# Second norm of a fused backbone layer: four MLP chunks split during the projection, its last four chunks worked token tile by token tile, three products kept back, and a fixed order

## The chip, the core and the metric

The kernel is one program on one core of a Trainium2 chip. It is written against a scheduling framework: the program is written as a stream of operations on named tiles, and the framework decides each engine's order of instructions and places the semaphores, except for operations that are pinned to the order in which they are written. The engines are TensorE (PE, with its weight loads shown as PEld), VectorE (DVE), ScalarE (ACT), GpSimd (POOL) and SyncE (SP, which here only issues the loads). The metric is the device time of one execution in microseconds, as the median of several runs.

## The reference

One layer of a diffusion backbone on 256 latent tokens of width 2048, with 256 context tokens: an attention branch and a pooling branch are merged by gates, projected by `w_o`, and followed by an MLP of width 8192. Everything is float32. The end of it, which is where the change lies:

```python
        mix = token_mixer(q, k_all, v_all, p[..., P_OFF:G_OFF], p[..., G_OFF:], lam, lam_init,
                          subln_w[l], pool_w[l], pool_scale[l], w_a_up[l], w_b_up[l], w_o[l])
        x = x + ga * mix
        x = x + gm * sq_relu_mlp(modulate(x, norm_mlp_w[l], sm, cm), w_ff1[l], w_ff2[l])
```

`token_mixer` ends with `(g_a * y_a + g_b * y_b) @ w_o`, `modulate(x, w, shift, scale)` is `rmsnorm(x, w) * (1 + scale) + shift`, and `sq_relu_mlp(h, w1, w2)` is `square(relu(h @ w1)) @ w2`. The vectors `ga`, `sm`, `cm` and `gm` are pieces of one product of the conditioning vector with a large weight `w_mod`. The second norm needs the whole row of 2048 features of `x`, so nothing of the MLP can start before the last column of the projection is done.

## The kernel before

**Tiles.** The 256 tokens are two token tiles of 128 (called token 0 and token 1, `t` in the code). A product of full precision is made of three products of a faster type: each operand is split into a high piece (a cast) and a low piece (the rest), and high x high, high x low and low x high are summed. Each weight comes as chunks of 128 x 1024 (512 KB). A chunk is loaded by SP into one of five `raw` buffers, its high piece is cast by ACT and its low piece subtracted by DVE (`load_next`, lines 196 to 240); the pieces lie in three buffers each (`whi`, `wlo`). A `raw` buffer is free for the next load once DVE has made the low piece. `wchunk` hands out the chunks in the order of the list `stream` and loads some ahead.

**The projection.** `w_o` is done in four groups `g` of 512 columns, each with eight chunks (called projection chunks 0 to 7; two slices of 128 features each) and one PSUM bank per token tile, `wo`. `xstat` (line 423) issues for each chunk twelve products of 512 columns: eight with the weight's high piece and four with its low piece, for both token tiles. The chunks of the last `last` of a group are instead worked token by token: first all products of token 0, then all of token 1. Before, `last` is 3 for the last group.

**The second norm.** `projected` (line 905) takes a finished bank: multiply by `ga` (tile `xtmp`), add to the residual `x1`, square on ACT with a row sum. `scaled` multiplies the new `x1` by the norm's scale into `yt`, 512 columns at a time. `norm2` sums the row sums of a token tile and makes the inverse root with two table functions on ACT and three tiny operations on DVE. `shifted(kp)` applies the root and adds the shift on one pair of feature slices (256 columns, "feature pair" `kp`, 0 to 7). `hidden2(kp)` turns that pair with PE transposes into the PSUM tile `h2T`, and `split` makes its high piece on ACT and its low piece on DVE, into `h2`.

**The first eighth of the MLP.** `ff1_first` (line 955) computes 1024 of the 8192 hidden features with the tokens as the stationary operand, from sixteen chunks of `w_ff1a` (MLP chunks 0 to 15, one slice of 128 features each). `products(k, t)` issues six products of 512 columns for chunk `k` and token tile `t`: three for each half `h` of the columns, into four banks `f1_{t}{h}` (shown as `f`).

**What sets the order.** While `ordered` is set, every operation of ACT and DVE that goes through the wrapper `Engine` is pinned, and its line reads L67; `ordered_pe` does the same for PE. Before, PE is pinned only in the last token-by-token group of the projection, and ACT and DVE are pinned from `projected(3, 0, ...)` to the second `products(1, 1)`. Operations of helpers that were bound before the flag was set, and all others, are placed by the framework. Between these stages run the late vectors: `late_gen` loads the weights of `ga`, `cm`, `sm` and `gm` in parts of 512 KB through the same `raw` buffers, one part whenever the `rate` of the chunks that were loaded has summed to one, and DVE multiplies and adds each part into `macc` (line 636). Before, `gm`, which is needed only at the very end, begins during the projection.

Of the kernel before, what the change touches and what calls it, by code (L numbers as in the profile page):

```python
# [17 lines left out]
P = 128  # L18
# [30 lines left out]
def layer(ctx: ExitStack, tc, a, out):  # L49
# [36 lines left out]
    def pairtile(name):  # L86
        return s16(name, [P, 2, 8, T], F32R)

    late = [None]
    credit = [0.0]  # L90
    credit_rate = [0.0]
# [81 lines left out]
    FIRST_AHEAD = 6  # L173
    x1s = []
    first = []

    def x1_tile():
        if not x1s:
# [17 lines left out]
    def load_next():  # L196
# [24 lines left out]
        raw = raw_chunk(src, n)  # L221
        if key == ("w_ff1a", 0):
            hi, lo = (pool.tile([P, n], F32R, tag="aT", name=nm, bufs=2) for nm in ("hi0", "lo0"))
        elif key == ("w_ff1a", 1):
            halves = [[work(nm, dt=F32R) for nm in ("hi1", "lo1")] for _ in range(2)]
            for h in range(2):
                split(*halves[h], raw[:, h * 512:h * 512 + 512])
            loaded.append((key, *zip(*halves)))
            return
        else:  # L230
            hi = pool.tile([P, n], F32R, tag="whi", name="whi", bufs=3)
            lo = pool.tile([P, n], F32R, tag="wlo", name="wlo", bufs=3)
# [4 lines left out]
        credit_rate[0] = rate  # L237
        while credit[0] >= 1.0:
            credit[0] -= 1.0
            next(late[0], None)  # L240

    def wchunk(*key, ahead=AHEAD):
        while len(loaded) < min(done[0] + 1 + ahead, len(stream)) or loaded[done[0]][1] is None:
# [179 lines left out]
    def xstat(w, banks, toks, nk=8, last=1, more=0):  # L423

# [3 lines left out]
        for ch in range(nk - last + 1):  # L428
# [6 lines left out]
            for group in groups:  # L435
                for part in range(2):
                    for i, kk, t in group:
                        k = 2 * (ch + i) + kk
                        h, tt = toks[t]
                        wt = chunks[i][part][:, kk * 512:kk * 512 + 512]  # L440
                        if part == 0:
                            pe.matmul(banks[t], tok(h, k, 0, tt), wt, start=k == 0, stop=False)  # L442
                            pe.matmul(banks[t], tok(h, k, 1, tt), wt, start=False, stop=False)  # L443
                        else:
                            pe.matmul(banks[t], tok(h, k, 0, tt), wt, start=False, stop=k == 2 * nk - 1)  # L445
            yield len(banks)
# [146 lines left out]


    ga_bc = s8("ga_bc", [P, D])
    mods = {}
    parts = []

    def late_gen():
        for name in ("ga", "cm", "sm", "gm"):  # L600
            if name == "ga":
                dst = ga_bc
            elif name == "gm":
                mods["gm"] = s8("gm_bc", [P, D])
                dst = mods["gm"]
            else:
                if "sb" not in mods:
                    mods["sb"] = s16("sb", [P, 2, D])
                dst = mods["sb"][:, 0 if name == "cm" else 1, :]
# [306 lines left out]
    def norm2(t):  # L916
        rv = small("rv", 1)
        vec.reduce_sum(rv, ssq[:, 4 * t:4 * t + 4], axis=AX.X)
        r2[t] = rsq(rv, 1, 1.0 / D)

    for g in range(4):
# [8 lines left out]
        next(late[0])  # L930
    flush()

    h2 = [pairtile(f"h2_{i}") for i in range(2)]
# [21 lines left out]
    def ff1_first(wo):  # L955
# [5 lines left out]
        bs = [[bank(f"f1_{t}{h}") for h in range(2)] for t in range(2)]  # L961
        chunks = {}

        def products(k, t):
            hi, lo = chunks[k]
            for h in range(2):
# [24 lines left out]
        scaled(3)  # L991
        shifted(2)
        hidden2(2)
        products(2, 1)
        for k in range(3, KT):
            if k % 2 == 0 and k < 14:
                shifted(k // 2 + 1)
                hidden2(k // 2 + 1)
            chunks[k] = wchunk("w_ff1a", k)
            for t in range(2):  # L1000
                products(k, t)
        at = pairtile("act")
# [177 lines left out]
```

## Time and profile before

| what | value |
|---|---|
| median of three runs | 1474.42 us |
| lowest and highest run | 1473.76 and 1475.06 us |
| the profiled execution's own time | 1475.86 us |
| its span, first to last instruction | 1474.0 us |
| PE busy | 1440.5 us, 98% of the span |
| DVE, ACT and POOL busy | 1000.8, 684.3 and 121.3 us |
| mean granted clock of PE | 0.990 |

A profile's timeline gives for each row the start and length in microseconds, the engine, the line of the kernel, the operation, what it writes and reads by the program's tile names, the shapes, how many equal ones are merged, and in square brackets how long the engine was idle before it and what released it. A table of stretches gives, for each stretch of time, each engine's busy time with its number of instructions, the clock that PE was granted, the share of the sixteen DMA engines that was busy, and GB/s. PE's ends are modelled: the next product starts before the shown end of the one ahead of it, so its pace is read from starts.

### The profile page before, as it was taken

Reading aid. Unit: us, or ns where it says so; the run is one execution under the profiler, and the core shown is the slowest. Engines: PE = TensorE matmul, PEld = TensorE weight load, DVE = VectorE, ACT = ScalarE, POOL = GpSimd, SP = SyncE. Lnnn points to the kernel's source line nnn. Section 1 sums busy time; section 2 is a strip of 40 time slices with the busy share of each in tenths; the row PEclk is TensorE's granted clock in tenths of the full one; section 3 lists DMA queues with packets and bytes.
Section 4 is the critical chain, followed back from the end, with each engine's and each line's share of the span. In section 5 each row is a group of like instructions: output and inputs, shape, how many; then the busy total and the mean of one; then the engine's idle time right before and its main releaser. Section 6 shows DMA issues by size and latency. Waiting matters only on the chain.

```text
span 1474.0 us, 19772 instructions
## 1 busy us (share of the span) xinstructions
PE 1440.5 (98%) x7466; PEld 1186.7 (81%) x7466; DVE 1000.8 (68%) x1243; ACT 684.3 (46%) x929; POOL 121.3 (8%) x120
## 2 busy tenths in 40 slices
PE   4999999999999999999999999999999999999998
PEld 2667887778878888888878888888888888888887
DVE  4667786768887687778776755666665555555675
ACT  4334346466554444544444555445354454544442
POOL 0001110101400000000001000001000000000260
PEclk7999999999999999999999999999999999999999
DMA  9996685435788879798746776677765655566554
GB/s 380 401 407 224 203 287 167 143 114 165 234 284 294 301 279 301 278 330 294 252 146 222 233 237 226 234 239 240 238 230 186 193 192 189 191 193 191 186 195 141
DMA packets 97440, 347.85 MB, mean 236 GB/s; under 512 B 11073, under 2 KB 11713, under 8 KB 97345
## 3 DMA queue, kind: packets, MB, share of 16 engines
q1 hardware_dynamic: 96768, 345.51, 69.4%
q8 instruction: 58, 0.95, 0.3%
q0 software_dynamic: 576, 1.08, 0.2%
q14 instruction: 38, 0.30, 0.1%
HBM read 344.45 MB, written 2.10 MB: 235 GB/s over the span
## 4 chain that ended last, share of the span: by engine, by line
PE 88%; DVE 6%; ACT 2%; DMA 2%; issue 1%; POOL 0%; DVEq 0%; SPq 0%; ACTq 0%; POOLq 0%
PE f L1029 14%; PE f L443 8%; PE f L442 8%; PE f L445 8%; PE f L1032 7%; PE pg L443 3%; PE pg L442 3%; PE pg L445 3%; PE w_k L67 3%; PE wo L442 2%; PE wo L445 2%; PE wo L443 2%; PE pyy L445 2%; PE pyy L442 2%; PE pyy L443 2%; DVE wlo L234 2%
## 5 line engine op out<-in xcount | busy, mean ns | idle before, releaser
L234 DVE TENSOR_TENSOR wlo<-raw,whi 128x1024 fp32r<-128x1024 f32 (+1 forms) x433 | 538.4, 1245 | 349.1 <-ACT whi L233 324.1
L233 ACT CAST whi<-raw 128x1024 fp32r<-128x1024 f32 (+1 forms) x433 | 452.8, 1047 | 555.6 <-PE f L443 184.6
L1029 PE MATMUL f<-h,whi 128*128 128x512 f32 x896 | 224.3, 392 | 0.0
L443 PE MATMUL f<-whi,act 128*128 128x512 f32 x512 | 199.3, 389 | 0.0
L442 PE MATMUL f<-whi,act 128*128 128x512 f32 x512 | 199.2, 389 | 0.0
L1029 PEld LDWEIGHTS f<-h,whi 128*128 128x128 f32 x896 | 161.8, 189 | 29.6
L636 DVE SCALAR_TENSOR_TENSOR macc<-raw,sil,macc 128x1024 f32<-128x1024 f32 x128 | 165.0, 1289 | 3.3 <-issue 2.6
L445 PE MATMUL f<-wlo,act 128*128 128x512 f32 x512 | 136.8, 389 | 0.0
L1032 PEld LDWEIGHTS f<-h,wlo 128*128 128x128 f32 x896 | 122.2, 190 | 8.7
L1032 PE MATMUL f<-h,wlo 128*128 128x256 f32 x896 | 124.9, 282 | 0.0
L445 PEld LDWEIGHTS f<-wlo,act 128*128 128x128 f32 x512 | 96.1, 188 | 19.9
L443 PEld LDWEIGHTS f<-whi,act 128*128 128x128 f32 x512 | 96.2, 188 | 19.8
L442 PEld LDWEIGHTS f<-whi,act 128*128 128x128 f32 x512 | 96.2, 188 | 19.7
L442 PE MATMUL pg<-whi,hL 128*128 128x512 f32 x256 | 101.4, 396 | 0.0
L443 PE MATMUL pg<-whi,hL 128*128 128x512 f32 x256 | 100.6, 393 | 0.0
L1040 POOL TENSOR_TENSOR rsq<-relu 128x512 f32<-128x512 f32 x28 | 29.2, 1042 | 543.3 <-ACT relu L1039 523.0
L445 PE MATMUL pg<-wlo,hL 128*128 128x512 f32 x256 | 68.6, 390 | 0.0
L443 PEld LDWEIGHTS pg<-whi,hL 128*128 128x128 f32 x256 | 48.5, 189 | 10.4 <-issue 0.2
L442 PEld LDWEIGHTS pg<-whi,hL 128*128 128x128 f32 x256 | 48.5, 189 | 10.3 <-issue 0.2
L445 PEld LDWEIGHTS pg<-wlo,hL 128*128 128x128 f32 x256 | 48.3, 189 | 10.2
L617 POOL MEMSET macc<- 128x1024 f32 x8 | 7.6, 955 | 461.6 <-DVE al L260 357.1
L442 PE MATMUL wo<-whi,mix 128*128 128x512 f32 x116 | 45.2, 390 | 0.0
(263 smaller groups left out, 2083.4 us busy)
## 6 DMA issues: line engine op xcount, KB each, us to landing
raw<-in_w_ff_dram SPq DMA_DIRECT2D x240, 512.0 KB, 4.0
raw<-in_w_m_dram SPq DMA_DIRECT2D x64, 512.0 KB, 9.7
raw<-in_w_ga_dram SPq DMA_DIRECT2D x32, 512.0 KB, 4.6
raw<-in_w_cm_dram SPq DMA_DIRECT2D x32, 512.0 KB, 4.4
raw<-in_w_gb_in_dram SPq DMA_DIRECT2D x32, 512.0 KB, 4.7
raw<-in_w_ga_in_dram SPq DMA_DIRECT2D x32, 512.0 KB, 5.0
raw<-in_w_sm_dram SPq DMA_DIRECT2D x32, 512.0 KB, 4.8
raw<-in_w_o_dram SPq DMA_DIRECT2D x32, 512.0 KB, 5.2
```

Of the source, the lines that this page charges most:

```text
L67: return (lambda *a, **k: pin(emit(*a, **k))) if self.flag[0] else emit
L233: act.copy(hi, raw)
L234: vec.tensor_sub(lo, raw, hi.bitcast(F32))
L442: pe.matmul(banks[t], tok(h, k, 0, tt), wt, start=k == 0, stop=False)
L443: pe.matmul(banks[t], tok(h, k, 1, tt), wt, start=False, stop=False)
L445: pe.matmul(banks[t], tok(h, k, 0, tt), wt, start=False, stop=k == 2 * nk - 1)
L617: gp.memset(acc, 0.0)
L636: pin(vec.scalar_tensor_tensor(acc, raw, sil[:, 0, k:k + 1], acc, ALU.mult, ALU.add))
L1029: pe.matmul(ps, hi[:, kk * P:kk * P + P], both(h2, k), start=k == 0, stop=False)
L1032: pe.matmul(ps[:, T:2 * T], lo[:, kk * P:kk * P + P], act_slice(h2, k, 0), start=False, stop=k == KT - 1)
L1040: gp.tensor_mul(sq, r, r)
```

## The change

The last group of the projection works its last four chunks (4 to 7) token by token instead of three. Chunk 4 gets pieces of its own (`pair`), so that its split does not wait for one of the three `whi` and `wlo` buffers. Of the MLP, four chunks instead of two are loaded and split before the norm begins; chunks 2 and 3 get a 16 KB tile of their own, `early`. Of token 1's projection the last three products (those with the weight's low piece for the last three feature slices) are kept back and issued between the transposes of token 0's feature pairs 0 and 1. The low pieces of those two pairs are made only after both transposes have been issued. After that, token 0 is multiplied with MLP chunks 0 to 3, with token 1's transposes inside the last of them, and then token 1. The pinned stretch of ACT and DVE now reaches to feature pair 2, the kept-back products stay pinned on PE, and every `shifted` is pinned wherever it stands. The second half of `h2` is taken when it is first needed, and `gm` is begun only with the chunks of the MLP. `scaled(3)` moves from behind `projected` to behind token 1's second pair.

```diff
@@ load_next @@
         if key == ("w_ff1a", 0):
             hi, lo = (pool.tile([P, n], F32R, tag="aT", name=nm, bufs=2) for nm in ("hi0", "lo0"))
+        elif key == ("w_o", 3, 4):
+            pair = s8("pair", [P, 2, 1024], F32R)
+            hi, lo = pair[:, 0, :], pair[:, 1, :]
+        elif key in (("w_ff1a", 2), ("w_ff1a", 3)):
+            i = 2 * (key[1] - 2)
+            if i == 0:
+                early.append(s16("early", [P, 4, 1024], F32R))
+            hi, lo = early[0][:, i, :], early[0][:, i + 1, :]
...
         while credit[0] >= 1.0:
             credit[0] -= 1.0
-            next(late[0], None)
+            if "gm" not in mods or mods["gm"] is not None or key[0] in ("w_ff1a", "w_ff1"):
+                next(late[0], None)
@@ xstat @@
+                        elif held_back is not None and group is groups[-1] and k >= 2 * nk - 3:
+                            held_back.append(partial(pe.matmul, banks[t], tok(h, k, 0, tt), wt, start=False,
+                                                     stop=k == 2 * nk - 1))
                         else:
                             pe.matmul(banks[t], tok(h, k, 0, tt), wt, start=False, stop=k == 2 * nk - 1)
@@ late_gen @@
             elif name == "gm":
+                mods["gm"] = None
+                yield
                 mods["gm"] = s8("gm_bc", [P, D])
@@ the projection @@
-        for ch, _ in enumerate(xstat(("w_o", g), bs, [(mix, 0), (mix, 1)], last=3 if g == 3 else 1, more=2 if g == 3 else 0)):
-            ordered_pe[0] = g == 3 and ch == 4
+        for ch, _ in enumerate(xstat(("w_o", g), bs, [(mix, 0), (mix, 1)], last=4 if g == 3 else 1, more=4 if g == 3 else 0,
+                                     held_back=held_back if g == 3 else None)):
+            ordered_pe[0] = g == 3 and ch == 3
@@ shifted, hidden2 @@
-            vec.scalar_tensor_tensor(yt[:, t, fs], yt[:, t, fs], r2[t], mods["sb"][:, 1, fs], ALU.mult, ALU.add)
+            pin(nc.vector.scalar_tensor_tensor(yt[:, t, fs], yt[:, t, fs], r2[t], mods["sb"][:, 1, fs], ALU.mult, ALU.add))
 
     def hidden2(kp, ts=(0, 1)):
+        turned2(kp, ts)()
+
+    def turned2(kp, ts):
+        if kp // 4 == len(h2):
+            h2.append(pairtile("h2_1"))
         pt = bank("h2T")
...
-        split(ht[:, 0, k8:k8 + 2, sl], ht[:, 1, k8:k8 + 2, sl], pt.rearrange("p (a t) -> p a t", t=T)[:, :, sl])
+        src = pt.rearrange("p (a t) -> p a t", t=T)[:, :, sl]
+        hi = ht[:, 0, k8:k8 + 2, sl]
+        act.copy(hi, src)
+        return lambda: vec.tensor_sub(ht[:, 1, k8:k8 + 2, sl], src, hi.bitcast(F32))
@@ ff1_first @@
+        for k in range(4):
+            chunks[k] = wchunk("w_ff1a", k, ahead=0)
         projected(3, 0, wo[0])
         norm2(0)
         shifted(0, (0,))
-        hidden2(0, (0,))
-        chunks[0] = wchunk("w_ff1a", 0, ahead=1)
-        products(0, 0)
+        shifted(1, (0,))
+        low = [turned2(0, (0,))]
+        for emit in held_back:
+            emit()
+        low.append(turned2(1, (0,)))
+        for emit in low:
+            emit()
         projected(3, 1, wo[1])
-        shifted(1, (0,))
-        hidden2(1, (0,))
-        chunks[1] = wchunk("w_ff1a", 1, ahead=1)
-        products(1, 0)
         norm2(1)
+        for k in range(3):
+            products(k, 0)
+        products(3, 0, (0,))
         shifted(0, (1,))
-        chunks[2] = wchunk("w_ff1a", 2, ahead=0)
-        products(2, 0)
+        shifted(1, (1,))
         hidden2(0, (1,))
-        products(0, 1)
-        shifted(1, (1,))
+        products(3, 0, (1,))
         hidden2(1, (1,))
-        products(1, 1)
-        ordered[0] = ordered_pe[0] = False
+        chunks[4] = wchunk("w_ff1a", 4, ahead=0)
+        for k in range(2):
+            products(k, 1)
         scaled(3)
         shifted(2)
         hidden2(2)
-        products(2, 1)
-        for k in range(3, KT):
+        ordered[0] = ordered_pe[0] = False
+        for k in range(2, 4):
+            products(k, 1)
+        for k in range(4, KT):
```

How this moves instructions is read from the built programs, engine by engine; the numbers behind tile names count buffers. PE at the end of the projection before (`wo_6357` is token 0, `wo_6358` token 1):

```order
L67 MATMUL wo_6357<-whi,mix_4785 128x512 x12
L67 MATMUL wo_6357<-wlo,mix_4785 128x512 x6
L67 MATMUL wo_6358<-whi,mix_4785 128x512 x12
L67 MATMUL wo_6358<-wlo,mix_4785 128x512 x6
L944 MATMUL h2T<-prm,yt 128x128 x2
L263 MATMUL f_00_6517<-hi_6464,h_0_6514 128x512
```

And in the changed kernel (`wo_6341` is token 0, `wo_6342` token 1):

```order
L67 MATMUL wo_6341<-pair,mix_4785 128x512 x2
L67 MATMUL wo_6341<-wlo,mix_4785 128x512 x6
L67 MATMUL wo_6342<-pair,mix_4785 128x512 x4
L67 MATMUL wo_6342<-whi,mix_4785 128x512 x12
L67 MATMUL wo_6342<-pair,mix_4785 128x512 x2
L67 MATMUL wo_6342<-wlo,mix_4785 128x512 x3
L966 MATMUL h2T<-prm,yt 128x128 x2
L67 MATMUL wo_6342<-wlo,mix_4785 128x512 x3
L966 MATMUL h2T<-prm,yt 128x128 x2
L274 MATMUL f_00_6505<-hi_6435,h_0_6503 128x512
```

Token 1 has 24 products instead of 18 here, of which 21 stand ahead of token 0's first transposes and three between them and the second pair. The next place is DVE from the last weight splits to token 1's multiply. Before:

```order
L260 TENSOR_TENSOR lo_6473<-raw,hi_6472 128x512
L234 TENSOR_TENSOR wlo<-raw,whi 128x1024
L67 TENSOR_TENSOR xtmp<-wo_6357,ga_bc 128x512
L67 TENSOR_TENSOR x_5801<-xtmp,x_5801 128x512
L903 TENSOR_TENSOR yt<-x_5801,sb 128x512
L67 TENSOR_REDUCE rv<-ssq_5820 128x1
...
L67 SCALAR_TENSOR_TENSOR yt<-yt,rq_y,sb 128x256
L938 SCALAR_TENSOR_TENSOR yt<-yt,rq_y,sb 128x256 x3
L67 TENSOR_TENSOR h_0_6514<-h2T,h_0_6514 128x2x128
L67 TENSOR_TENSOR xtmp<-wo_6358,ga_bc 128x512
```

And in the changed kernel:

```order
L271 TENSOR_TENSOR lo_6444<-raw,hi_6443 128x512
L244 TENSOR_TENSOR wlo<-raw,whi 128x1024
L244 TENSOR_TENSOR early<-raw,early 128x1024 x2
L67 TENSOR_TENSOR xtmp<-wo_6341,ga_bc 128x512
L67 TENSOR_TENSOR x_5801<-xtmp,x_5801 128x512
L67 TENSOR_REDUCE rv<-ssq_5820 128x1
...
L955 SCALAR_TENSOR_TENSOR yt<-yt,rq_y,sb 128x256 x2
L67 TENSOR_TENSOR h_0_6503<-h2T,h_0_6503 128x2x128 x2
L67 TENSOR_TENSOR xtmp<-wo_6342,ga_bc 128x512
```

The two early splits now stand between the projection's last split and token 0's multiply, the shifts of later features (L938) and `scaled(3)` (L903) have left the stretch, and token 1's multiply stands behind both low pieces instead of one.

More of the change, by code (lines that the diff above doesn't have):

```diff
@@ L87, in pairtile @@
         return s16(name, [P, 2, 8, T], F32R)
+    mods = {}
     late = [None]
@@ L175, in layer @@
     first = []
+    early = []
     def x1_tile():
@@ L421, in xmm, with xstat @@
             mm3(ps, tok(h, k, 0, t), tok(h, k, 1, t), hi[:, sl], lo[:, sl], first, last)
-    def xstat(w, banks, toks, nk=8, last=1, more=0):
+    def xstat(w, banks, toks, nk=8, last=1, more=0, held_back=None):
         for ch in range(nk - last + 1):
@@ L595, in layer @@
     ga_bc = s8("ga_bc", [P, D])
-    mods = {}
     parts = []
@@ L919, in norm2 @@
         r2[t] = rsq(rv, 1, 1.0 / D)
+    held_back = []
     for g in range(4):
         bs = [bank(f"wo{t}") for t in range(2)]
-        for ch, _ in enumerate(xstat(("w_o", g), bs, [(mix, 0), (mix, 1)], last=3 if g == 3 else 1, more=2 if g == 3 else 0)):
-            ordered_pe[0] = g == 3 and ch == 4
+        for ch, _ in enumerate(xstat(("w_o", g), bs, [(mix, 0), (mix, 1)], last=4 if g == 3 else 1, more=4 if g == 3 else 0,
+                                     held_back=held_back if g == 3 else None)):
+            ordered_pe[0] = g == 3 and ch == 3
         if g < 3:
@@ L931, in layer @@
     flush()
-    h2 = [pairtile(f"h2_{i}") for i in range(2)]
+    h2 = [pairtile("h2_0")]
     def shifted(kp, ts=(0, 1)):
@@ L962, in ff1_first, with products @@
         chunks = {}
-        def products(k, t):
+        def products(k, t, hs=(0, 1)):
             hi, lo = chunks[k]
-            for h in range(2):
+            for h in hs:
                 whi, wlo = (w[h] if isinstance(w, tuple) else w[:, h * 512:h * 512 + 512] for w in (hi, lo))
                 mm3(bs[t][h], tok(h2, k, 0, t), tok(h2, k, 1, t), whi, wlo, k == 0, k == KT - 1)
+        for k in range(4):
+            chunks[k] = wchunk("w_ff1a", k, ahead=0)
         projected(3, 0, wo[0])
@@ L998, in ff1_first @@
                 hidden2(k // 2 + 1)
-            chunks[k] = wchunk("w_ff1a", k)
+            if k > 4:
+                chunks[k] = wchunk("w_ff1a", k)
             for t in range(2):
```

## The prediction

> **What bounds the kernel now.** I read the page first: TensorE (PE) is the bound, so only time in which PE does not run at its full pace can be won.
>
> ```profile
> span 1474.0 us, 19772 instructions
> PE 1440.5 (98%) x7466; PEld 1186.7 (81%) x7466; DVE 1000.8 (68%) x1243; ACT 684.3 (46%) x929; POOL 121.3 (8%) x120
> ```
>
> Then the table of stretches around the second norm, cut at the events of the next view (columns: stretch, its length, busy time of each engine with instructions, granted clock, DMA share, GB/s).
>
> ```profile
> 743.22:751.38 8.16, 8.16 (x37) 6.57 (x35) 4.33 (x10) 1.66 (x5) 0.00 (x0) 1.00 0.66 243
> 751.38:755.00 3.62, 3.02 (x13) 2.19 (x13) 3.62 (x9) 0.60 (x2) 0.00 (x0) 1.00 0.00 0
> 755.00:758.50 3.50, 1.58 (x7) 0.76 (x5) 3.21 (x8) 3.11 (x6) 0.00 (x0) 1.00 0.00 0
> 758.50:762.00 3.50, 3.49 (x8) 2.80 (x9) 3.40 (x8) 1.08 (x3) 0.00 (x0) 0.51 0.67 202
> ...
> 766.44:772.00 5.56, 5.56 (x30) 4.67 (x29) 3.00 (x3) 3.17 (x4) 0.00 (x0) 1.00 0.07 10
> ```
>
> PE is full until 751.38 and again from 766.44. Between them it loses time in two ways: it waits, and for 3.5 us its clock is 0.51. PE's own timeline names the waits (start, length, what, idle before and its releaser):
>
> ```profile
> 743.22 2.88 PE L67 MATMUL wo<-whi,mix 128*128 128x512 f32 x12
> 745.94 1.52 PE L67 MATMUL wo<-wlo,mix 128*128 128x512 f32 x6
> 747.30 2.88 PE L67 MATMUL wo<-whi,mix 128*128 128x512 f32 x12
> ...
> 751.68 0.44 PE L944 MATMUL h2T<-prm,yt 128*128 128x128 f32 x2
> 752.58 0.50 PE L263 MATMUL f<-hi,h 128*128 128x512 f32 x1 [0.46 <-ACT h L67]
> ...
> 757.25 0.73 PE L263 MATMUL f<-whi,h 128*128 128x512 f32 x2 [1.41 <-ACT whi L67]
> 758.51 0.80 PE L264 MATMUL f<-wlo,h 128*128 128x512 f32 x1 [0.52 <-DVE wlo L67]
> ...
> 763.33 0.50 PE L263 MATMUL f<-hi,h 128*128 128x512 f32 x1 [0.46 <-ACT h L67]
> ...
> 764.83 0.38 PE L944 MATMUL h2T<-prm,yt 128*128 128x128 f32 x2
> ...
> 765.28 0.39 PE L264 MATMUL f<-lo,h 128*128 128x512 f32 x1
> ```
>
> Twelve products start every 2.72 us (743.22 to 745.94): 0.227 each. A pair of transposes with the product behind it takes 0.45 (764.83 to 765.28), so a pair costs 0.22. The MLP products of the gap, counted by the same table for the tile f alone:
>
> ```profile
> 751.38:766.44 15.06, 11.03 (x36) 7.57 (x36) 0.00 (x0) 0.00 (x0) 0.89 0.32 106
> ```
>
> At full pace 36 products (8.16) and four pairs (0.88) take 9.04 us; they took 15.06. **The stage loses 6.02 us**, the most that can be won here. Of it the eight products at half clock (758.50 to 762.00) are 8 x (0.43 - 0.227) = about 1.7; the rest is waiting.
>
> What PE waits for shows in VectorE's (DVE's) timeline: first token 0's norm, then weights whose splits stand behind it.
>
> ```profile
> 747.50 0.69 DVE L67 TENSOR_TENSOR xtmp<-wo,ga_bc 128x512 f32<-128x512 f32 x1 [2.67 <-PE wo L67]
> ...
> 751.14 0.48 DVE L67 SCALAR_TENSOR_TENSOR yt<-yt,rq_y,sb 128x256 f32<-128x256 f32 x1
> ...
> 752.73 0.42 DVE L67 TENSOR_TENSOR h<-h2T,h 128x256 fp32r<-128x256 f32 x1
> ...
> 757.24 1.22 DVE L67 TENSOR_TENSOR wlo<-raw,whi 128x1024 fp32r<-128x1024 f32 x1
> ...
> 758.45 2.35 DVE L234 TENSOR_TENSOR wlo<-raw,whi 128x1024 fp32r<-128x1024 f32 x2
> ...
> 761.29 0.48 DVE L67 SCALAR_TENSOR_TENSOR yt<-yt,rq_y,sb 128x256 f32<-128x256 f32 x1
> ```
>
> ScalarE (ACT) copies the turned tile in between:
>
> ```profile
> 752.15 0.37 ACT L67 CAST h<-h2T 128x256 fp32r<-128x256 f32 x1 [1.63 <-PE h2T L944]
> ```
>
> From the first multiply (747.50) to the shifted tile (751.14 + 0.48) a norm takes 4.12; from a transpose (751.68) to the first product that uses it (752.58) 0.90. The chunks split at 757.24 and 758.45 hold PE up (1.41 and 0.52), and token 1's norm stands in the same queues: its shift comes at 761.29.
>
> **The change part by part.** I set out the new order on before's clock. No product is added or removed; PE is full up to the projection's last group, so that group's start moves by one chunk (12 products) to 743.22 - 2.72 = 740.50.
>
> *Four last chunks token by token, and the kept-back products.* Token 0's 24 products end at 740.50 + 24 x 0.227 = 745.94. Its multiply started 0.20 after the group's end before (747.50 against 747.30), so now at 746.14; the first shifted tile is ready at 750.26, the second 0.40 later. Token 1's first 21 products cover until 750.70: the transposes find their tile ready, with 0.44 to spare. The three kept-back products (0.68) and the second pair then cover the 0.90 that the first piece needs for its copy: the first MLP product can start at about 751.73, its input is there at 751.60. The two waits at 751.68 and 752.58 go.
>
> *Four early chunks.* 24 products of token 0 (four chunks) now need no weight work, so the waits of 1.41 and 0.52 go. Their cover was never there; the price moves into the projection, where two more splits cost ACT 2 x 1.05 and DVE 2 x 1.22. DVE was busy 4.33 of 8.16 us and ACT 1.66 of 8.16 at its end, so both have room, if the chunks land in time:
>
> First the view of the loads' line from 734 to 746 us, then rows of the timelines of DVE, ACT and SP with the order of splits and issues:
>
> ```profile
> DMA to landing us min/median/max: 4.0/4.7/5.3
> ```
>
> ```profile
> 730.00 1.22 DVE L234 TENSOR_TENSOR wlo<-raw,whi 128x1024 fp32r<-128x1024 f32 x1
> ...
> 739.81 1.23 DVE L234 TENSOR_TENSOR lo<-raw,hi 128x1024 fp32r<-128x1024 f32 x1 [0.38 <-ACT hi L233]
> ```
>
> ```profile
> 738.72 1.05 ACT L233 CAST hi<-raw 128x1024 fp32r<-128x1024 f32 x1 [0.55 <-DMA raw<-in_w_ff1a_dram]
> ```
>
> ```profile
> 734.32 0.33 SPq L115 DMA_DIRECT2D raw<-in_w_ff1a_dram  x1
> ...
> 741.06 0.33 SPq L115 DMA_DIRECT2D raw<-in_w_ff1a_dram  x1
> 742.20 0.33 SPq L115 DMA_DIRECT2D raw<-in_w_ff1a_dram  x1
> ...
> 744.86 0.33 SPq L115 DMA_DIRECT2D raw<-in_w_ff1a_dram  x1
> ```
>
> A load waits in SP's queue for the first free raw buffer: MLP chunk 3's went out at 741.06, when chunk 0's split ended (739.81 + 1.23). Projection chunk 4 now has its own home, so its split runs ahead of chunk 2's, and each later load moves up by one split: chunk 0 is then loaded after the split that ended at 731.22, plus chunk 4's own 1.2 on DVE, say 732.2; it lands 4.4 later (734.32 to 738.72 before), is cast by 737.9 (a square stands ahead of it on ACT) and is split by 739.2. Chunk 3 goes out then, lands by 743.9 to 744.5 (4.7 to 5.3) and is split (1.05 + 1.22) by 746.2 to 746.8. Token 0's multiply stands behind that on DVE and wants to start at 746.14: it is late by 0.1 to 0.7 against 0.44 to spare. I take 0.1 of waiting, with 0 and 0.3 as its bounds.
>
> *Token 1.* On DVE its multiply now stands behind token 0's two low pieces. The second pair starts at 751.60; its copy (0.47 later, 0.37 long) and low piece (0.42) end at 752.89. So the norm runs to 752.90 + 4.12 = 757.02. PE gets there after 22 products and a pair: 756.81. Wait 0.27 (with 0.06 to start). The copy behind it (0.90 from 757.08) makes the first token-1 product wait 0.10. Ahead of feature pair 2, the two scalings (0.61 each) and shift stand on DVE behind one weight split: 759.04 + 1.8 + 1.2 + 0.5 = about 762.5, PE comes at 762.4: 0.2. Sum 0.57; bounds 0 and about 1.6 (each of three up to the 0.46 to 0.52 of the rows above).
>
> *Fixed shifts.* Before, the shifts of later features ran in DVE's holes long ahead; now each stands just before its transposes. For five pairs the second token's transposes can wait up to 0.40 - 0.13 = 0.27: 0 to 1.35, taken as 0.5.
>
> *The last modulation vector.* Its loads and multiply-adds leave the projection and come later. No path: it was done at 1103.8 and is first needed at 1393.7; four parts at one in four chunks of 2.72 us (line 165's rate) are some 45 us. The rows are from the view of that tile:
>
> ```profile
> L1072 POOL TENSOR_TENSOR acc<-acc,gm_bc x8: 1295/1788/2278, 1393.7 to 1429.8; 128x512 f32<-128x512 f32 x8
> L660 ACT COPY gm_bc<-late x4: 577/585/588, 910.5 to 1103.8; 128x512 f32<-128x512 f32 x4
> ```
>
> *The clock.* The same table shows the half clock twice more after the start, each time behind a stretch in which PE worked under half:
>
> ```profile
> 273.50:277.00 3.50, 1.54 (x9) 0.88 (x7) 3.46 (x5) 0.34 (x1) 0.00 (x0) 1.00 0.91 277
> 277.00:281.00 4.00, 3.41 (x11) 2.91 (x12) 2.40 (x5) 2.80 (x7) 0.00 (x0) 0.57 0.91 333
> ...
> 437.50:441.00 3.50, 1.59 (x6) 0.78 (x5) 3.35 (x4) 3.03 (x4) 0.00 (x0) 1.00 0.87 268
> 441.00:445.00 4.00, 4.00 (x12) 3.13 (x11) 1.83 (x3) 0.64 (x1) 2.55 (x4) 0.57 0.97 360
> ```
>
> With 1.54, 1.59 and here 1.58 busy of 3.50 it fell; with 3.02 of 3.62 (751.38) it did not. No stretch of the new order has over 0.4 of waiting, so I count the 1.7 us as won. The Trainium skill, "TensorE: Matmul & The Clock Gate" (its part on the clock gate), says otherwise: half rate returns after an idle window of about 3.4 us, and gaps under some 3 us are safe. The longest wait here is 1.41, so by that rule it would not be the waits that slow the clock. The three rows stand against the rule.
>
> **Sum.** New waits 0.10 + 0.57 + 0.50 = 1.17. Saving 6.02 - 1.17 = 4.85, say 4.9. The profiled execution took 1475.86 (span 1474.0 and 1.86 around it) and would take 1471.0; the median of the runs, 1474.42, is 1.44 lower, so 1469.5. With the bounds (0 to 3.25 of new waits) and 0.65 of spread between runs, the forecast's own range is 1467.8 to 1472.
>
> **The rivals.**
> A: the slow clock is not caused by these waits and stays. For it: only three cases; against it: all three have the same share. Saving 4.9 - 1.7 = 3.2: 1471.2. The page named above would give this.
> B: token 1's norm stays exposed, since the fixed order puts both low pieces and the whole chain in one queue; each of three waits at 0.5 and all five later pairs in full: 0.1 + 1.5 + 1.35, saving 3.1: 1471.3. Against it: DVE has holes in 755 to 770.
> C: the change does not bring the chunks early. If chunk 3's load waits for projection chunk 6's split (as the 742.20 load did), it lands at 747.5, is split at 749.8, and token 0's multiply is 3.7 late: a wait of 3.2 and a slow stretch of 1.7, all that was won: 1474.4.
> D, slower: the same queue, one step worse. If chunk 3 waits for projection chunk 7's split (as the load at 744.86 did), it lands at 750.1, its split ends at 752.4, the multiply is 6.3 late: PE waits 5.8 and pays one or two slow stretches, 7.5 to 9.2 against 4.9: 1477 to 1479, say 1478. It decides from a landing at about 747.6 on.
>
> **How the numbers follow.** Forecast 0.67, A 0.08, B 0.08, C 0.11, D 0.06. Below 0.2% (2.95 us) a measurement of this kernel can hardly tell a difference: faster means under 1471.47, slower over 1477.37. Faster: nearly all of the forecast (0.66), and most of A and B (0.12): 0.78. Slower: D, 0.05. Same: the rest, 0.17. The range reaches from the forecast's lower end, with a little for run spread, to short of C: 1467.5 to 1472.8; it leaves out C and D and some at the edges.
>
> **What would show it.** Right: no wait over 0.4 us on PE between the projection's last group and the fifth MLP chunk, no half clock there, the first transposes within 5 us of token 0's last projection product, and the early splits ended before the multiply. C or D: DVE idle ahead of the early splits, with their load as releaser. B: waits on shifted tiles. A: half clock without waits ahead of it. A span that shrinks by less than this stage does would mean that the price is paid elsewhere.

## The result and the profile after

| | before | changed |
|---|---|---|
| median | 1474.42 us | 1470.83 us |
| lowest and highest of nine runs each | 1472.08 to 1476.98 | 1466.40 to 1472.39 |
| ratio, with its 95% interval | | 0.9972 (0.9960 to 0.9983) |
| the profiled execution's own time | 1475.86 us | 1469.82 us |

The change makes the kernel 3.6 us faster by the medians, 2.5 to 5.9 by the interval. The forecast was 1469.5 in a range of 1467.5 to 1472.8.

The page of the changed kernel, its span and busy times:

```profile
span 1467.8 us, 19774 instructions
PE 1437.1 (98%) x7466; PEld 1183.6 (81%) x7466; DVE 1000.2 (68%) x1243; ACT 683.5 (47%) x929; POOL 121.3 (8%) x120
```

To compare kernels I take one stretch in each: from the first product of projection chunk 4 to the first product of the MLP's second eighth. It holds everything that the change touches on PE. In the table of stretches, the first row is the stretch and the second all that comes behind it (length, then the busy times with instructions, then the granted clock after POOL's column). Before:

```profile
740.50:804.65 64.15, 61.16 (x274) 49.23 (x272) 43.88 (x64) 27.08 (x40) 0.90 (x1) 0.97 0.56 180
804.65:1473.97 669.32, 664.81 (x3353) 566.76 (x3351) 409.92 (x423) 309.12 (x373) 66.74 (x50) 1.00 0.64 208
```

The same two of the changed kernel, and from the stretch two finer pieces, around token 0's transposes and its MLP products:

```profile
738.95:798.45 59.50, 59.50 (x273) 47.47 (x272) 40.14 (x60) 24.98 (x37) 0.89 (x1) 1.00 0.53 175
798.45:1467.75 669.30, 664.81 (x3353) 566.66 (x3351) 415.64 (x428) 309.19 (x373) 66.74 (x50) 1.00 0.65 212
...
749.15:750.20 1.05, 1.05 (x8) 0.87 (x7) 0.23 (x1) 0.37 (x1) 0.00 (x0) 1.00 0.00 0
750.20:755.40 5.20, 5.20 (x26) 4.04 (x24) 3.09 (x10) 1.69 (x5) 0.00 (x0) 1.00 0.01 3
```

The stretch fell from 64.15 to 59.50, by 4.65 us. PE is busy in every microsecond of it and the clock is 1.00 throughout. Behind it nothing moved: 669.32 and 669.30, the same 664.81 of PE, though the last modulation vector now falls into that part (by the view of its tile, its last piece is copied at 1152.4 and it is first used at 1387.5, so it is still far ahead of its use). PE's timeline of the changed kernel around the norm shows no bracket (a product is shown 0.39 long and the next starts 0.227 behind it, so a delay of up to some 0.16 would not show, either as a bracket or as idle time):

```profile
738.95 1.07 PE L67 MATMUL wo<-pair,mix 128*128 128x512 f32 x4
...
744.39 0.84 PE L67 MATMUL wo<-pair,mix 128*128 128x512 f32 x3
...
748.47 0.85 PE L67 MATMUL wo<-wlo,mix 128*128 128x512 f32 x3
749.15 0.38 PE L966 MATMUL h2T<-prm,yt 128*128 128x128 f32 x2
749.29 0.94 PE L67 MATMUL wo<-wlo,mix 128*128 128x512 f32 x3
750.07 0.38 PE L966 MATMUL h2T<-prm,yt 128*128 128x128 f32 x2
750.20 0.48 PE L274 MATMUL f<-hi,h 128*128 128x512 f32 x1
...
755.15 0.40 PE L274 MATMUL f<-early,h 128*128 128x512 f32 x1
755.40 0.44 PE L966 MATMUL h2T<-prm,yt 128*128 128x128 f32 x2
...
756.30 0.50 PE L274 MATMUL f<-hi,h 128*128 128x512 f32 x1
```

Token 0's transposes (749.15) start one pace behind the projection's products and 4.76 us after token 0's last product was issued and PE had turned to token 1 (744.39), the kept-back three run behind them, and the first MLP product starts at 750.20. Of the five waits before (0.14, 0.46, 1.41, 0.52, 0.46; the first, ahead of the transposes at 751.68, is too short for a bracket, and all five make up the 2.99 that PE was not busy) none is left, nor is the half clock. DVE's timeline shows the early splits done and out of the way:

```profile
735.49 1.23 DVE L244 TENSOR_TENSOR lo<-raw,hi 128x1024 fp32r<-128x1024 f32 x1
...
740.51 1.22 DVE L244 TENSOR_TENSOR early<-raw,early 128x1024 fp32r<-128x1024 f32 x1
742.38 1.23 DVE L244 TENSOR_TENSOR early<-raw,early 128x1024 fp32r<-128x1024 f32 x1 [0.65 <-ACT early L243]
744.59 0.69 DVE L67 TENSOR_TENSOR xtmp<-wo,ga_bc 128x512 f32<-128x512 f32 x1 [0.97 <-PE wo L67]
...
773.05 1.23 DVE L244 TENSOR_TENSOR wlo<-raw,whi 128x1024 fp32r<-128x1024 f32 x1 [1.49 <-ACT whi L243]
774.20 0.87 DVE L955 SCALAR_TENSOR_TENSOR yt<-yt,rq_y,sb 128x256 f32<-128x256 f32 x2
```

The second early split ends at 743.61, and token 0's multiply (744.59) then waits 0.97 for the projection, not the other way round. The last two rows are one of the later feature pairs: DVE stands idle for 1.49 us, makes a weight's low piece, and only then the shift.

### The profile page after: what moved, and what is told of

The parts are those of the page before. It is cut to its first block, busy times and chain, and to the rows that moved or that the text cites. A ratio compares the mean times of both kernels' runs of the same rounds, so it can differ in the third digit from the quotient of the medians.

```text
span 1467.8 us, 19774 instructions
## 1 busy us (share of the span) xinstructions
PE 1437.1 (98%) x7466; PEld 1183.6 (81%) x7466; DVE 1000.2 (68%) x1243; ACT 683.5 (47%) x929; POOL 121.3 (8%) x120
## 4 chain that ended last, share of the span: by engine, by line
PE 91%; DVE 4%; ACT 2%; DMA 1%; issue 1%; POOL 0%; DVEq 0%; SPq 0%; ACTq 0%; POOLq 0%
PE f L1061 14%; PE f L454 8%; PE f L453 8%; PE f L459 8%; PE f L1064 7%; PE pg L454 4%; PE pg L453 4%; PE pg L459 4%; PE w_k L67 3%; PE wo L453 2%; PE wo L454 2%; PE pyy L453 2%; PE pyy L459 2%; PE pyy L454 2%; PE wo L459 2%; PE v L459 2%
## 5 line engine op out<-in xcount | busy, mean ns | idle before, releaser
L1086 DVE TENSOR_TENSOR acc<-f,acc 128x512 f32<-128x512 f32 x48 | 30.9, 686 | 19.6 <-PE f L459 19.6
```

Of the source, the lines that this page charges most:

```text
L1086: vec.tensor_add(acc[:, t, gs], bs[t], acc[:, t, gs])
```

## The experiments

All times of "the stretch" are the one defined above. The first column of the table gives the kernel's stretch, the second PE's waits in it, the third the whole time (median where there were several runs).

| kernel | stretch | waits | whole time |
|---|---|---|---|
| before | 64.15 | 0.14, 0.46, 1.41, 0.52, 0.46, half clock | 1474.42 |
| changed | 59.50 | none | 1470.83 |
| shifts left free | 58.63 | none | 1470.06 |
| no kept-back products | 59.92 | 0.24 | 1469.59 (one run) |
| two early chunks | 63.64 | 1.15, 0.53, half clock | 1473.74 (one run) |
| four early chunks on the kernel before | 66.66 | 3.54, 0.46, 0.46, 0.23, half clock twice | 1477.73 (one run) |
| last three chunks instead of four | 60.59 | 0.81 | 1473.97 (one run) |
| shift one feature pair ahead | 58.65 | none | 1468.42 |

**The shifts left free.** In the changed kernel, `shifted` goes back to the operation that the framework may place:

```diff
-            pin(nc.vector.scalar_tensor_tensor(yt[:, t, fs], yt[:, t, fs], r2[t], ...))
+            vec.scalar_tensor_tensor(yt[:, t, fs], yt[:, t, fs], r2[t], ...)
```

> The changed kernel, but with the shifts of the later feature pairs (2 to 7 outside the pinned stretch) left to the framework again. Measured for the changed kernel: from the first product of projection chunk 4 to the first product of the second eighth of the MLP 59.50 us (before 64.15). Theory F (each fixed shift stands just ahead of its transposes and makes the second token's pair wait): the waits of about 0.25 at four later pairs go, the stretch becomes 58.5 to 58.8, and the time falls by 0.7 to 1.0 below the changed kernel, some 1469.9 against 1474.4 before. Rival G (the fixed shifts keep DVE free for the splits, so freeing them moves the wait to a weight or a low piece): the stretch stays at 59.4 to 59.8.

Measured: median 1470.06 (1467.61 to 1471.21), ratio to the kernel before 0.9970 (0.9959 to 0.9981). The stretch is 0.87 shorter than the changed kernel's. A later feature pair on PE:

```profile
774.02 0.39 PE L276 MATMUL f<-whi,h 128*128 128x512 f32 x1
774.25 0.60 PE L966 MATMUL h2T<-prm,yt 128*128 128x128 f32 x4
774.60 0.47 PE L274 MATMUL f<-whi,h 128*128 128x512 f32 x1
```

The same pair of the changed kernel:

```profile
774.49 0.39 PE L274 MATMUL f<-whi,h 128*128 128x512 f32 x1
774.82 0.74 PE L966 MATMUL h2T<-prm,yt 128*128 128x128 f32 x4
775.32 0.48 PE L275 MATMUL f<-wlo,h 128*128 128x512 f32 x1
```

From the product ahead to the product behind, 0.83 against 0.58: 0.25 per pair, though PE shows no bracket. It fits the two shifts of DVE above: the first is done at 774.68, the second at 775.07, and the second token's transposes stand behind it. That term of the forecast was right in kind.

**The kept-back products.** The three products are issued with the rest of token 1's:

```diff
-                                     held_back=held_back if g == 3 else None)):
+                                     held_back=None)):
```

> The changed kernel without the three kept-back products: all 24 products of token 1 stand ahead of the first transposes, and both pairs of transposes follow each other. Theory F (the kept-back products cover the copy of the first turned tile): the first MLP product waits 0.5 to 0.7 for that copy (0.90 from transpose to product, less the second pair), the stretch grows from 59.50 to 60.0 to 60.2. Rival G (they only move work): it stays within 0.15 of 59.50.

Measured: the stretch is 59.92, 0.42 more. PE's timeline has the wait that they covered:

```profile
750.23 0.50 PE L274 MATMUL f<-hi,h 128*128 128x512 f32 x1 [0.24 <-ACT h L67]
```

It is the copy of the turned tile, as expected, but 0.24 instead of 0.5 to 0.7, and the stretch stays just under theory F's 60.0. The products' gain is seen in the stretch and small, far inside the spread of whole times (this one run was faster than the changed kernel's median).

**Two early chunks.** MLP chunks 2 and 3 are split where the norm is, as in the kernel before; everything else stays changed:

```diff
-        elif key in (("w_ff1a", 2), ("w_ff1a", 3)):
-            ...
-    more=4 if g == 3 else 0
+    more=2 if g == 3 else 0
-        for k in range(4):
+        for k in range(2):
             chunks[k] = wchunk("w_ff1a", k, ahead=0)
...
         projected(3, 1, wo[1])
+        chunks[2] = wchunk("w_ff1a", 2, ahead=0)
         norm2(1)
+        chunks[3] = wchunk("w_ff1a", 3, ahead=0)
```

> The changed kernel with only MLP chunks 0 and 1 split early; chunks 2 and 3 are loaded into the common buffers and split inside token 1's norm, as before. Theory F (the early splits remove the waits for weights, and with them the half clock): PE waits again for chunk 2 and chunk 3, high and low pieces, 3 to 4 us in all without any single wait over 2, and a stretch of half clock of 3.4 us follows (1.7 more): the stretch is 63 to 65 us. Rival R (the half clock needs an idle time of about 3.4 us at a stretch): the same waits, but no half clock, 62.5 to 63.3.

Measured: 63.64, 4.1 of the 4.65 lost again. PE's timeline, then the stretches around it:

```profile
754.34 0.73 PE L269 MATMUL f<-whi,h 128*128 128x512 f32 x2 [1.15 <-ACT whi L67]
755.60 0.55 PE L270 MATMUL f<-wlo,h 128*128 128x512 f32 x1 [0.53 <-DVE wlo L67]
```

```profile
752.00:755.90 3.90, 2.23 (x9) 1.22 (x8) 1.89 (x3) 1.91 (x4) 0.00 (x0) 1.00 0.00 0
755.90:759.32 3.42, 3.38 (x8) 1.87 (x7) 2.50 (x6) 1.27 (x3) 0.00 (x0) 0.50 0.44 153
759.32:764.00 4.68, 4.68 (x23) 3.69 (x23) 2.96 (x5) 1.69 (x3) 0.00 (x0) 1.00 0.42 117
```

The waits come back at the same two products with the same releasers, 1.68 in all and so less than the 3 to 4 expected, and 3.42 us of half clock directly behind them. Together they are 1.68 + 1.7 = 3.4; the other 0.7 has no bracket, and in part it is products at half clock that stand further apart than their 0.43. The rival that the clock has nothing to do with these waits falls, and so does rival R: no wait here came near 3.4 us.

**Four early chunks alone**, on the kernel before: no `pair`, the last three chunks token by token, the old order. As in the change, the second half of `h2` is taken only when it is first needed; the diff shows the lines on the early chunks alone.

```diff
+        elif key in (("w_ff1a", 2), ("w_ff1a", 3)):
+            ...
+            hi, lo = early[0][:, i, :], early[0][:, i + 1, :]
-    more=2 if g == 3 else 0
+    more=4 if g == 3 else 0
-        chunks[0] = wchunk("w_ff1a", 0, ahead=1)
+        chunks[0] = wchunk("w_ff1a", 0, ahead=0)
-        chunks[1] = wchunk("w_ff1a", 1, ahead=1)
+        chunks[1] = wchunk("w_ff1a", 1, ahead=0)
```

> The kernel before with only this of the change: MLP chunks 2 and 3 are loaded and split early into their own tile. Projection chunk 4 keeps the common buffers, the last three chunks go token by token, nothing is kept back. Theory F (rival C of the prediction is real: without a home of its own for chunk 4 every load comes one split later, and the early split holds token 0's norm on DVE): chunk 3's split ends 2 to 4 us after token 0's last projection product, the first transposes wait 2.5 to 4 us, a half clock may follow, the waits of 1.41 and 0.52 are gone, and the stretch is 63 to 66. Rival G (the early splits alone bring the gain): no wait over 1 us at the first transposes, the stretch is 60.5 to 61.5.

Measured: 66.66, longer than the kernel before, and 1477.73 for the whole. The size is near what rival C asked for, but the cause is another. PE's wait, and DVE's timeline ahead of it:

```profile
754.45 0.69 PE L952 MATMUL h2T<-prm,yt 128*128 128x128 f32 x2 [3.54 <-DVE yt L67]
```

```profile
745.60 1.23 DVE L240 TENSOR_TENSOR early<-raw,early 128x1024 fp32r<-128x1024 f32 x1 [0.27 <-ACT early L239]
746.87 0.69 DVE L67 TENSOR_TENSOR xtmp<-wo,ga_bc 128x512 f32<-128x512 f32 x1
...
749.49 0.16 DVE L67 TENSOR_REDUCE rv<-ssq 128x1 f32<-128x4 f32 x1 [0.47 <-ACT x1sq L67]
750.05 2.36 DVE L240 TENSOR_TENSOR wlo<-raw,whi 128x1024 fp32r<-128x1024 f32 x2 [0.40 <-PE wo L67]
752.33 0.15 DVE L67 SCALAR_TENSOR_TENSOR rq_t<-rq_y 128x1 f32<-128x1 f32 x1
752.39 1.22 DVE L240 TENSOR_TENSOR wlo<-raw,whi 128x1024 fp32r<-128x1024 f32 x1
```

PE turned from token 0 to token 1 at 746.67, and token 0's multiply started 0.20 later, the same as in the kernel before (747.50 after 747.30): even without `pair` the early chunks came just in time, because PE turns later here. The changed kernel without `pair` was not run; an estimate from the two traces says that its early chunks would be late. Counted from the first product of projection chunk 4, the last early split ends at 6.96 here (746.83 less 739.87) and at 4.66 with `pair` in the changed kernel (743.61 less 738.95), where token 0's multiply starts at 5.64. What PE waits for are three other splits (3.6 us), set by the framework between the tiny operations of the norm; their line is L240, so they are not pinned. By the code these are MLP chunks 4 to 6, next in the stream once chunks 0 to 3 have homes of their own, and the projection sets their buffers free just then. In the changed kernel chunk 4's split is pinned behind token 1's transposes and none enters the norm; that its pin keeps the others out too is argued from the code, not tested. The two waits of 1.41 and 0.52 are gone here as well, and the long one brought two slow windows:

```profile
750.60:754.08 3.48, 0.31 (x2) 0.00 (x0) 3.41 (x7) 1.12 (x2) 0.00 (x0) 1.00 0.52 177
754.08:757.49 3.41, 2.58 (x7) 1.79 (x8) 3.41 (x8) 0.37 (x1) 0.00 (x0) 0.50 0.94 310
757.49:760.91 3.42, 3.42 (x10) 2.54 (x9) 1.50 (x4) 0.72 (x2) 0.00 (x0) 0.50 0.03 12
```

**Three chunks token by token** in the changed kernel:

```diff
-    last=4 if g == 3 else 1
+    last=3 if g == 3 else 1
-            ordered_pe[0] = g == 3 and ch == 3
+            ordered_pe[0] = g == 3 and ch == 4
```

> The changed kernel with only the last three projection chunks worked token by token (three products of token 1 still kept back, chunk 4 still in its own tile). Theory F (the fourth chunk is needed so that token 1's products cover token 0's norm): token 1 has 15 products (3.40 us) ahead of the transposes against a norm of 4.12 less the 0.20 at its start, so the first transposes wait about 0.6, and the stretch from projection chunk 4 to the second eighth of the MLP grows from 59.50 to 60.0 to 60.3. Rival G (three chunks would have been enough, the kept-back products take up the wait): it stays within 0.15 of 59.50. No half clock by either.

Measured: 60.59, 1.1 more, with one wait, for token 0's shifted tile:

```profile
753.29 0.44 PE L966 MATMUL h2T<-prm,yt 128*128 128x128 f32 x2 [0.81 <-DVE yt L955]
```

With 18 products of token 1, of which three are kept back, the norm's chain of some 4.1 us is not covered; with 24 it is. The fourth chunk is worth a little more than expected (0.81 against 0.6), and no half clock follows a wait of this size.

**The kernel before, profiled three more times**, unchanged, to see whether its half clock at the norm is there in every execution or only in some.

> The kernel before once more, for its clock. Theory W (the clock is set in windows of 3.41 us that run freely, and halves for one window after a window with about 1.7 us or more of PE idle, 1.48 and less being harmless so far): the waits at the second norm are the same 1.41 and 0.52 within 2.7 us, and whether half clock follows depends on where the window's border falls; in each run the three places (near 277, 440 and 758 us) follow that rule, and among three looks at least one has no half clock at the norm, with a stretch of 62.4 to 62.7 instead of 64.15. Rival S (the waits always halve it, as the prediction counted): half clock at the norm in all three looks, 64.0 to 64.3.

> The same as the look before it. Theory W: half clock at the norm only where one window holds 1.7 us or more of the waits. Rival S: always.

> The same as the two looks before it. Theory W: half clock at the norm only where one window holds 1.7 us or more of the waits. Rival S: always.

Measured: stretches of 64.11, 64.12 and 64.17, each with the waits of 1.41 and 0.52 to 0.53 and the half clock behind them. The second of the three, on PE:

```profile
758.97 0.73 PE L263 MATMUL f<-whi,h 128*128 128x512 f32 x2 [1.41 <-ACT whi L67]
760.23 0.54 PE L264 MATMUL f<-wlo,h 128*128 128x512 f32 x1 [0.53 <-DVE wlo L67]
```

So four of four profiled executions of the kernel before pay it, as rival S has it; theory W's look without it did not come. That does not show that every execution pays it. In all four the half clock near 441 us came first, 317.44 us or 93 windows of 3.413 ahead, and an execution without that one was not seen. The timed runs' mean clocks bear on it too: one slow window lowers the mean by 0.0012 (half of 3.41, over 1474), and two of the 37 timed runs of the kernel before with a clock on record read 0.995. Of the 13 profiles only one without any slow window amid the program reached that (the first with free shifts); with one window it was 0.994. Unless these two had a shorter half clock at their start than any profile, they did not pay at the norm; how many others did not is open.

**The changed kernel and the free shifts again**, and a third version that keeps the fixed order but writes each shift one feature pair ahead of its transposes:

```diff
+        shifted(3)
...
             if k % 2 == 0 and k < 14:
-                shifted(k // 2 + 1)
                 hidden2(k // 2 + 1)
+                if k < 12:
+                    shifted(k // 2 + 2)
```

> The changed kernel once more, beside the version with free shifts, to see whether the time agrees with the stretch. By the stretch (59.5 against 64.15, nothing else moved) the changed kernel is 4.6 us faster than before; by the first medians 3.6. Theory F (the stretch is all that the change moves; the rest of the difference is run spread from stages ahead of it): the stretch is again 59.4 to 59.7, the part behind it 669.3 as in every run so far, and the ratio's interval holds 0.9969. Rival H (the change costs about 1 us elsewhere): a part of the trace outside the stretch is longer by about 1 us than in the looks at the kernel before.

> The changed kernel with free shifts once more, on the same chip as the run before it. Theory F: a stretch of 58.5 to 58.8, and a median 0.5 to 1.3 below the changed kernel's. Rival H (the gain in the stretch is given back): a median within 0.3 of it.

> The changed kernel with the later shifts still fixed, but each written one feature pair earlier, behind the transposes of the pair ahead of it. Theory F (what costs is only that a fixed shift stands just ahead of its transposes, not that it is fixed): the waits at the later pairs go as with free shifts, a stretch of 58.4 to 58.8. Rival G (any fixed order costs): 59.2 or more.

Measured on one chip against 26 runs of the kernel before (median 1474.60): changed 1471.08, ratio 0.9977 (0.9966 to 0.9988); free 1468.70, 0.9960 (0.9947 to 0.9974); one pair ahead 1468.42, 0.9965 (0.9952 to 0.9977). The stretches are 59.59, 58.63 and 58.65. The pair of the third version, on PE and on DVE:

```profile
777.29 0.39 PE L276 MATMUL f<-whi,h 128*128 128x512 f32 x1
777.52 0.60 PE L966 MATMUL h2T<-prm,yt 128*128 128x128 f32 x4
777.87 0.47 PE L274 MATMUL f<-whi,h 128*128 128x512 f32 x1
```

```profile
774.61 0.87 DVE L955 SCALAR_TENSOR_TENSOR yt<-yt,rq_y,sb 128x256 f32<-128x256 f32 x2
```

The shifts are done at 775.48, two microseconds ahead of the transposes, and the pair takes 0.58 again. So it is not the fixed order that costs, but the place: right before its consumer, behind a weight split that itself waits for ACT. Both versions have a stretch 0.9 shorter than the changed kernel's and a lower median in the same comparison (by 2.4 and 2.7, of which the trace accounts for 0.9; 2.4 is also more than the 0.5 to 1.3 expected). Over all timed runs the means differ by 1.4 and 1.3, give or take 1.0 and 1.6, so more than the 0.9 is not shown. Both are faster than the kernel before.

Of the changed kernel's own question: behind the stretch all 13 profiles have 669.28 to 669.32, so no cost is hidden there. Ahead of it they spread from 738.50 to 742.21 (740.50 to 742.21 in the kernel before, 738.95 and 740.46 in the changed one), too wide to see or exclude a microsecond.

## Why the prediction was right, term by term

The forecast of 4.85 us rests on a stage loss of 6.02 less new waits of 1.17. At full pace the stretch would take 64.15 - 6.02 = 58.13; it took 59.50, so the new waits are 1.37 and the saving 4.65. The mechanism was right; that the sum came so close (1.37 against 1.17) was partly luck, because terms erred in opposite directions.

| term | predicted | measured |
|---|---|---|
| waits and half clock that go | 6.02 | all five waits and the half clock gone |
| early splits hold token 0's multiply | 0.10 | 0: the split ended 0.97 ahead |
| token 1's norm | 0.57 | with the row above at most 0.50 (58.63 - 58.13) |
| fixed shifts | 0.50 | 0.87 (59.50 - 58.63) |
| sum of new waits | 1.17 | 1.37 |

*The stage loss.* The 6.02 rests on starts and stands, but it was split wrongly. Eight products 0.203 slower are 1.62, not 1.7, and the rest is not all waiting that a bracket shows: the five waits are 2.99. The other 1.4 lies where no bracket reaches; some 0.8 of it, five times 0.16, because a bracket counts only from the modelled end of the product ahead.

*Early chunks.* Chunk 0's low piece was forecast to end at 739.2 and chunk 3 to be split by 746.2 to 746.8. The changed kernel runs 1.55 earlier from the stages ahead (738.95 against 740.50), so on before's clock chunk 0's low piece ended at 736.72 + 1.55 = 738.27 and the last early split at 745.16. SP's and ACT's rows of chunk 3's load and cast:

```profile
736.74 0.33 SPq L116 DMA_DIRECT2D raw<-in_w_ff1a_dram  x1
```

```profile
741.30 1.05 ACT L243 CAST early<-raw 128x1024 fp32r<-128x1024 f32 x1 [1.01 <-DMA raw<-in_w_ff1a_dram]
```

The chain was as forecast (the load goes out when chunk 0's split has ended, 4.5 us to its landing), only a microsecond sooner. (The forecast's 732.2 for chunk 0's load should read 732.4, 731.22 + 1.2; it went out at 729.85 + 1.55 = 731.40.) So the wait taken as 0.10 did not occur.

*Token 1.* Forecast were waits of 0.27, 0.10 and 0.20. PE shows none: 0.25 from the product at 755.15 to the transposes at 755.40, against a pace of 0.23. All that is left for these places and the early splits, 0.50, includes a slightly slower pace of products: from 753.06 to 755.15 they start every 0.232, not 0.227, which makes 0.2 over the 36 that were counted. How the other 0.3 divides was not resolved.

*Fixed shifts.* This is the term that was mis-sized. I took 0.5 of a possible 1.35, as if the split ahead of a shift were in the way only at some pairs. Starts of the same products in the changed kernel's second profile and in the third version show what each pair cost: 0.26, 0.25 and 0.26 at feature pairs 5 to 7, nearly all of the possible 0.27, 0.12 at pair 4 and 0.01 at pair 3. What I did not ask is what stands in front of the shift on DVE: a split that is bound to ACT's cast.

*Whole time.* Between the profiled executions the span fell by 6.22: 1.55 ahead of chunk 4, 4.65 in the stretch, 0.02 behind it. The first of these differs from one execution of the same kernel to the next; in this pair one has a half clock near 277 us and the other not (last section). The medians differ by 3.6 and, in the second comparison, 3.5; both intervals hold 4.65 (2.5 to 5.9, and 1.8 to 5.0). Over all timed runs on record, 46 of the kernel before and 21 of the changed one, the means differ by 4.0 (3.0 to 4.9), which holds it too, so a gain below that of the stretch is not shown. If there is one, a half clock at the norm in some executions only remains a possible reason: the mean clocks of the timed runs, 0.9924 and 0.9931, differ by 0.0007 where one window in every run would make 0.0012, but they scatter too much (0.0007 either way) to decide.

*The rivals.* A (the slow clock stays) fell: no half clock in the stretch after, and it returns with the waits in two experiments. B (token 1 exposed, 1471.3): the later pairs cost 0.87 of the 1.35 in its price, the three waits of 0.5 did not come. C (chunk 3 late) and D (chunk 7's split) were not seen; DVE waited for PE, not the reverse. The experiment meant to bring C about lost its time to splits inside the norm chain, a danger that no rival named, though the prediction's own rows show two such splits (758.45) in token 1's norm before.

## What to carry to other kernels

When a stage waits for weights, look for what keeps their loads back: a few chunks with homes of their own let every later load move up, and a few products kept back cover the latency of a copy. A fixed order must place each producer a full step ahead of its consumer, and ask what stands in front of it in its queue; whatever is left unpinned can be set into the chain that one wanted to protect. Two short waits close together can cost nearly as much again in clock as in waiting (1.7 behind 1.93 here), so count them with the clock that follows.

## What the runs showed of the clock that I had not expected

Amid the program the half clock lasted about 3.42 us or twice that, and it depended on how much of such a window PE was idle, not on one long wait: 1.41 + 0.52 at the norm was enough in four of four executions of the kernel before, 1.15 + 0.53 in the experiment with two early chunks, while 0.81 alone was not. Within one execution the slow stretches start whole multiples of 3.413 us apart. With the 13 traces cut into windows of that length on these borders, from 60 us on, windows with less than 1.5 us idle were followed by full clock (but for one that was itself at half clock, in the run with four early chunks alone), those with 1.93 or more always by half clock, and those between went either way. Whether a transpose counts as work there was not tested.

The same wait does not always have the same effect. Ahead of a transpose in the attention stage every one of these kernels waits 2.54 to 2.55 us. Before, PE's row and the stretch behind it:

```profile
277.59 1.09 PE L477 MATMUL qkT<-prm,qraw 128*128 128x128 f32 x4 [2.54 <-ACT e L709]
```

```profile
277.40:281.00 3.60, 3.41 (x11) 2.91 (x12) 2.00 (x4) 2.40 (x6) 0.00 (x0) 0.55 0.88 333
```

And in the changed kernel:

```profile
277.39 0.63 PE L491 MATMUL qkT<-prm,qraw 128*128 128x128 f32 x4 [2.55 <-ACT e L724]
```

```profile
277.40:281.00 3.60, 3.60 (x18) 3.04 (x19) 1.81 (x4) 2.10 (x5) 0.00 (x0) 1.00 0.94 330
```

The first is followed by half clock, the second not; the unchanged kernel, profiled again, did it in some executions and not in others. That fits windows which run on regardless of the program, so that a wait falls into one of them or across two. The Trainium skill, "TensorE: Matmul & The Clock Gate" (Part 1, the HAM clock gate), calls the activity window free-running, and with that the rows agree; it puts the return to half rate after a whole idle window of about 3.4 us, and there the rows differ: 1.68 to 1.93 us of idle time in parts was enough, and the measurement decides. Why the window at the norm fell so in all four profiles of the kernel before is open; the constant 317.44 us to the slow window near 441 suggests that this one decides it, which was not tested.
